# Squares of the first feed-forward layer on ScalarE, its sums on VectorE, a smaller stock of weight planes, and head blocks squared one per group

## The chip, the cores and the metric

The kernel runs on one core of one Trainium2 chip. The metric is the device time of one execution in microseconds (us). Three executions of the kernel before took 1282.55, 1283.82 and 1284.52 us, so its median is 1283.82 us.

## The reference

An encoder block: layer norm, an input projection, two attention branches (a two-dimensional neighbourhood attention and a windowed grouped attention), gating, an output projection, a second layer norm, and a squared-ReLU MLP. The change touches the stretch from the output projection to the end of the MLP's first layer:

```
attn_out = mixed @ w_out + b_out
h = layer_norm(ALPHA * h + attn_out, ln1_g, ln1_b)
u = jnp.square(jax.nn.relu(h @ w_ff1 + b_ff1))      # first layer, 1024 -> 4096
ffn_out = u @ w_ff2 + b_ff2                         # second layer, 4096 -> 1024
h = layer_norm(ALPHA * h + ffn_out, ln2_g, ln2_b)
```

There are 1024 tokens of width 1024.

## The kernel before

All five engines follow an order that is written out in the program: each engine takes its instructions in that order, and waits where a semaphore asks for it.

**Output projection (`out_mm`, TensorE, about 560 to 660 us).** It goes in eight groups g of 128 tokens. Each group has two halves of 24 matmuls. Between the two quarters of the second half stand the eight transposes of the group before, `turn(g - 1)` (L1374), which need that group normalised (`normalise`, L176, on ScalarE, after statistics on VectorE and a power on GpSimd). `turn_evac` takes the transposes out of PSUM (six of eight on ScalarE, L1385), and `combine` turns the tokens into the first layer's operands.

**First layer (`ff1_mm`, L1471).** It is done by Strassen's method in Winograd's form: for each of 16 blocks p of 256 hidden units there are seven products i, in the order `STEPS` = 1, 2, 6, 5, 7, 3, 4. One product is 12 matmuls of 128x512 in float16, because each operand is held as a high and a low plane. The weight planes of a product are made by ScalarE (`hi1`, L1673, a scaled copy) and VectorE (`lo1`, L1677, the rest); for products 6, 5, 7 and 4 VectorE first makes a sum of weight blocks (`sums1`, L1647 and L1662). `tick()` makes the planes of one product, and `prep_to(n)` ticks until the stock reaches product n. The table `PREP` says up to where for the first products, a formula with `LOOK` for the later ones. Blocks 0 to 3 are the head blocks: their products 1 and 2 run between the last groups of the projection, and their weights lie in the upper halves of the operand tiles (`raws`, loaded by `head_w`). The remaining products stand in `seq`: (0,6), (1,6), (0,5), (1,5), (0,7), (0,3), (0,4), (1,7), (1,3), (1,4), then 6, 5, 7, 3, 4 of blocks 2 and 3, then all seven of blocks 4 to 15. I write (p,i) for product i of block p, and n for its place in `seq`.

**Scales.** A block's weights are scaled by their norm: `squares1` (L1423, ScalarE, one 128x2048 instruction), a tiny matmul (L1428), `scale1` on VectorE (L1433) and GpSimd (L1434).

**Results.** `snap` (L1562, ScalarE) copies a partial sum out of PSUM, which lets the next product accumulate into that bank. `act_fn` adds a second partial sum to it on VectorE (L1581), and `settle()`, one or two products later, runs the rest: max with zero and square in one VectorE instruction (L1584), and the store. The fourth result (A21) has its ReLU and square on ScalarE (L1578, L1579). `u_sums` makes four sums of the squared blocks for the second layer, one after each of the next products (two in block 1), on GpSimd (L1685).

**Second layer (L1937).** It starts when the last products of block 15 are out; its operands are loaded, and cast by ScalarE (L1799) and VectorE (L1802).

Of the kernel before, what the change touches and what calls it, by code (L numbers as in the profile page):

```python
# [13 lines left out]
AF = mybir.ActivationFunctionType  # L14
ALU = mybir.AluOpType
# [46 lines left out]
LO_ON = (2, 3, 4, 5), (1, 3, 5)  # L62
RS = 3, 3.5, 4.5, 5.5
HI_AT = -1
PREP = 5, 6, 7, 8, 8, 9, 11, 12, 13, 14, 15, 17, 18, 20, 22
HI_ACT = (2, 3, 4, 5), ()
ST0=2
NO_DVE = ()
# [22 lines left out]
def encoder_block(ctx, tc, x, w_in, w_br, w_out, w_ff1, w_ff2, par, rows, rpbp,  # L91
                  ident_d, masks_d, rope_d, out):
    nc = tc.nc
    PE, ACT, DVE, POOL = nc.tensor, nc.scalar, nc.vector, nc.gpsimd
# [61 lines left out]
    def dma_w(src):  # L156
        raw = wp.tile([P, 8, P], F32, tag="raw", name="raw", bufs=2)
        nc.sync.dma_start(raw, src)
        return raw
# [633 lines left out]
    with tc.manual_schedule(engines=MANUAL):  # L793
        raws = [dma_w(gate_w(i, 8 - N_AHEAD)) for i in range(2)]
# [480 lines left out]
        for f in range(8):  # L1275
            for half in range(2):
# [8 lines left out]
                g, h = (f, 1) if half == 0 else (f + 1, 0)  # L1285
# [26 lines left out]
    raws = {}  # L1312
# [109 lines left out]
    def squares1(p, raw):  # L1422
        ACT.activation(junk1, raw.rearrange("p r c k n -> p (r c k n)"), AF.Square, accum_out=sq1[:, p:p + 1],  # L1423
                       saturate=False)

    def sum_sq1(p, tag):
        ps = psum(tag)
        PE.matmul(ps[:, 0:2], ones, sq1[:, p:p + 1].to_broadcast([P, 2]), start=True, stop=True)  # L1428
        return ps

    def scale1(p, ps):
        t = tw1[:, 2 * p:2 * p + 2]
        DVE.scalar_tensor_tensor(out=t, in0=ps[:, 0:2], scalar=Q_MIN, in1=cv, op0=ALU.max, op1=ALU.mult)  # L1433
        POOL.tensor_tensor(out=sw1[:, 2 * p:2 * p + 2], in0=t, in1=pw, op=ALU.pow)  # L1434
# [14 lines left out]
    def head_w(p):  # L1449

        nc.sync.dma_start(raws[p], w_ff1[p])
# [36 lines left out]
    with tc.manual_schedule(engines=MANUAL):  # L1488
# [10 lines left out]
        for g in range(NCG):  # L1499
            out_mm(g, 0, 0, 8)  # L1500
            if 2 <= g + 1 < NCG:
                split_mx(g + 1)
            if g + 2 < NCG:
                pre(g + 2)
            out_evac(g, 0)
            out_mm(g, 1, 0, 4)
            if g:
                turn(g - 1)
            out_mm(g, 1, 4, 8)
            if g == 4:  # L1510
                head_ps = [sum_sq1(p, "o") for p in range(2)]
            if g == 7:
                head_ps += [sum_sq1(p, "o") for p in range(2, 4)]
            if g:
                turn_evac(g - 1)
            if g == 3:
                for p in range(2):
                    squares1(p, raws[p])
            if g == 5:
                head_split(0, 1)  # L1520
                head_split(0, 2)
            if g == 6:
                for p in range(2, 4):
                    squares1(p, raws[p])
            out_evac(g, 1)
            if g == 0:
                bound(bound_sum())
            ln1_norm(g)
            if g < 5:
                late(g + 3)  # L1530
            if g == 5:
                op_places("S1", "S2")
            if g:
                combine(g - 1)
            if g == 2:
                for p in range(2):
                    head_w(p)
            if g == 4:
                for p in range(2):
                    scale1(p, head_ps[p])  # L1540
            if g == 5:
                for p in range(2, 4):
                    head_w(p)
            if g == 6:
                head_split(1, 1)
                head_split(1, 2)
            if g == 7:
                for p in range(2, 4):
                    scale1(p, head_ps[p])
# [24 lines left out]
        def act_fn(p, i, n, ps, add, f):  # L1574

            u = us[p, n] = ufree.pop(0)
            if add is None:
                ACT.activation(u, ps, AF.Relu, bias=f_bias(p, f), scale=w_back(p))  # L1578
                ACT.activation(u, u, AF.Square)  # L1579
                return  # L1580
            DVE.scalar_tensor_tensor(out=u, in0=ps, scalar=w_back(p), in1=add, op0=ALU.mult, op1=ALU.add)  # L1581

            def rest_of():
                DVE.scalar_tensor_tensor(out=u, in0=u, scalar=0.0, in1=u, op0=ALU.max, op1=ALU.mult)  # L1584
                store_u(p, i, u)
            waiting.append(rest_of)

# [47 lines left out]
        raw1, sums = {}, {}  # L1635
# [44 lines left out]
        def u_sums(p):  # L1680

            u11, u12, u21, u22 = (us[p, n] for n in ("A11", "A12", "A21", "A22"))

            def one(i, out, a, b, op=ALU.subtract):
                POOL.tensor_tensor(out=out, in0=a, in1=b, op=op)  # L1685
                store_u(p, i, out)
            return [lambda: one(7, u11, u11, u21), lambda: one(5, u21, u21, u22, ALU.add),
                    lambda: one(6, u22, u22, u11),
                    lambda: (one(3, u12, u12, u22), ufree.extend((u11, u21, u22, u12)))]
# [25 lines left out]
        def prep_to(n):  # L1715
            while n_prep[0] < min(n, len(seq)):
                tick()
# [46 lines left out]
        def residual_rows1():  # L1764
            for r in range(2):
                nc.sync.dma_start(xts[0][:, r, :], rr_d[2 + r].partition_broadcast(P))
# [117 lines left out]
                tring.insert(0, slot2("q2"))  # L1884

        tails = []
        LOOK = 9
        n_res = 0
        for n, (p, i) in enumerate(seq):
            prep_to(PREP[n] if n < len(PREP) else n + min(LOOK, 5 + n // 3))  # L1890
            if n == 0:
                comb_hi("A22")
            elif n == 1:
                comb_lo("A22")
            elif n == 2:
                more_tw()
            if n == 12:
                xts.append(x1p.tile([P, 2, D], F32, tag="m", name="rr"))
                xts.append(x0p.tile([P, 4, 512], F32, tag="m", name="rst"))
                residual_rows1()  # L1900
            if n in (11, 14):
                scale1(n // 3 + 1, sum_sq1(n // 3 + 1, "s"))
            ff1_mm(p, i)
            if n in (8, 11):
                squares1(n // 3 + 2, raw1[n // 3 + 2])
            if (p, i) == (NP - 1, 6):

                t = hp.tile([P, 2, 4, 512], F32, tag="h3", name="stg")
                gring.extend(t[:, x] for x in range(2))
                load_s(0)  # L1910
            for f in tails[:2 if p == 1 else 1]:
                tails.pop(0)()
            after1(p, i)
            if p == NP - 1:
                turn_over(i)
            if i == 4:
                tails.extend(u_sums(p))
            if n > 12 and n % 4 == 0 and n_res < 2 * NCG + 2:
                if n_res >= 2:
                    residual()  # L1920
                if n_res < 2 * NCG:
                    residual_load(n_res, xn1_d)
                n_res += 1
# [141 lines left out]
        for n in range(L3):  # L2065
            i = idx(n)
# [150 lines left out]
```

## Time and profile before

| quantity | value |
|---|---|
| median of three executions | 1283.82 us |
| the profiled execution | 1282.07 us |
| its span, first to last instruction | 1280.3 us |
| TensorE busy | 1249.4 us, 98% |
| VectorE busy | 993.2 us, 78% |
| ScalarE busy | 703.9 us, 55% |
| GpSimd busy | 409.1 us, 32% |
| mean granted TensorE clock | 0.998 |

A row of the timeline gives the start in us from the span's start, the duration, the engine, the source line, the operation, output and input tiles, the shape, and a count; in square brackets stands how long the engine was idle before it, and which instruction ended that idle time. PE is TensorE, DVE is VectorE, ACT is ScalarE, POOL is GpSimd, SPq is SyncE's DMA queue. Instructions of one engine overlap by 0.08 to 0.16 us, so the distance from start to start is the price of one in a row of them.

### The profile page before, as it was taken

The numbers are of one execution on the slowest core, as the hardware profiler recorded it, in microseconds if no ns is written. First come the engines' busy times: TensorE is split into PE (matmuls) and PEld (weight loads), VectorE is DVE, ScalarE is ACT, GpSimd is POOL, SyncE is SP. The second block draws the span as 40 slices with busy tenths as digits, with TensorE's granted clock in tenths as the row PEclk, the third lists the DMA queues.
The fourth block names the chain that finished last, engine by engine and source line by source line (L and its number), as shares of the span: only waits on it lengthen the run. The fifth ranks groups of instructions, "written<-read, shape, count | busy, mean of one in ns | idle before, by whom it ended". The sixth has DMA issues, their size and how long they took to land.

```text
span 1280.3 us, 16490 instructions
## 1 busy us (share of the span) xinstructions
PE 1249.4 (98%) x5946; PEld 915.5 (72%) x5946; DVE 993.2 (78%) x1369; ACT 703.9 (55%) x1088; POOL 409.1 (32%) x372
## 2 busy tenths in 40 slices
PE   8999999999999999999998999999999999999997
PEld 6788887877778788888773444444447888888885
DVE  7667889777778964445679989999958677797778
ACT  6448778667675455424556655555535542333346
POOL 4343322112110003437510457676632001111207
PEclk9999999999999999999999999999999999999999
DMA  6535667465566326552442466566547644534223
GB/s 235 169 127 142 155 156 163 112 157 126 129 146 194 109 106 235 189 186 105 182 155 75 143 201 214 206 215 206 173 148 285 251 158 168 221 143 179 107 107 132
DMA packets 166066, 211.55 MB, mean 165 GB/s; under 512 B 110432, under 2 KB 112224, under 8 KB 159712
## 3 DMA queue, kind: packets, MB, share of 16 engines
q1 hardware_dynamic: 165152, 209.72, 50.8%
q8 instruction: 46, 0.75, 0.3%
q10 hardware_dynamic: 832, 0.79, 0.2%
q14 instruction: 36, 0.29, 0.1%
HBM read 128.59 MB, written 56.18 MB: 144 GB/s over the span
## 4 chain that ended last, share of the span: by engine, by line
PE 76%; DVE 11%; ACT 4%; issue 3%; DMA 2%; POOL 2%; SPq 1%; DVEq 0%; POOLq 0%; ACTq 0%
PE ps_mm L316 17%; PE ps_mm L1937 7%; PE ps_s L1937 6%; PE ps_mm L1471 5%; PE ps_t L1471 5%; PE ps_o L1937 5%; PE ps_o L1471 5%; PE ps_t L1937 5%; PE ps_s L1471 2%; PE ps_o L744 2%; PE ps_mm L977 2%; PE ps_o L308 1%; PE ps_t L308 1%; PE ps_t L306 1%; PE ps_o L307 1%
## 5 line engine op out<-in xcount | busy, mean ns | idle before, releaser
L316 PE MATMUL ps_mm<-hT,whi 128*128 128x512 f32 x832 | 269.7, 398 | 6.6 <-DVE kl L429 4.0
L1471 PEld LDWEIGHTS <-tw 128*128 128x128 f16 x1248 | 122.0, 99 | 149.0 <-issue 4.1
L316 PEld LDWEIGHTS ps_mm<-hT,whi 128*128 128x128 f32 x832 | 155.2, 188 | 41.1 <-ACT ss L659 3.9
L316 PE MATMUL ps_mm<-hT,wlo 128*128 128x512 f32 x416 | 165.5, 398 | 1.0 <-DVE wlo L810 1.0
L1685 POOL TENSOR_TENSOR usl<-usl 128x512 f32<-128x512 f32 x64 | 100.3, 1567 | 120.4 <-ACT usl L1579 112.0
L659 ACT ACTIVATE ss<-ss,sk 128x384 f32<-128x384 f32 (+1 forms) x128 | 74.3, 582 | 57.7 <-DVE sk L641 34.5
L1799 ACT CAST t<-stg 128x2048 fp32r<-128x2048 f32 x28 | 53.6, 1913 | 81.8 <-PE ps_o L1937 46.4
L1956 POOL TENSOR_TENSOR acc<-acc,rst 128x512 f32<-128x512 f32 x16 | 28.0, 1749 | 212.8 <-DMA rst<-xr_d 184.7
L1937 PE MATMUL ps_mm<-t,t 128*128 128x512 f32 x384 | 89.9, 390 | 0.0
L1269 POOL TENSOR_TENSOR mx<-sg 128x512 f32<-128x512 f32 x16 | 33.5, 2091 | 176.4 <-DVE sg L1268 176.4
L1937 PE MATMUL ps_s<-t,t 128*128 128x512 f32 x384 | 89.6, 389 | 0.0
L316 PEld LDWEIGHTS ps_mm<-hT,wlo 128*128 128x128 f32 x416 | 78.3, 188 | 14.0 <-DVE wlo L810 1.5
L1471 PE MATMUL ps_t<-hS,tw 128*128 128x512 f16 x372 | 85.4, 379 | 1.8 <-ACT sn L1562 1.7
L1937 PEld LDWEIGHTS ps_mm<-t,t 128*128 128x128 f32 x384 | 72.0, 188 | 15.2 <-DVE t L1802 0.2
L1937 PEld LDWEIGHTS ps_s<-t,t 128*128 128x128 f32 x384 | 72.1, 188 | 14.9
L1802 DVE TENSOR_TENSOR t<-stg,t 128x2048 fp32r<-128x2048 f32 x28 | 66.9, 2388 | 12.1 <-ACT t L1799 12.1
L1677 DVE SCALAR_TENSOR_TENSOR tw<-ts,c,tw 128x512 f16<-128x512 f32 x61 | 72.0, 1185 | 2.8 <-ACT tw L1673 2.7
L1937 PE MATMUL ps_t<-t,t 128*128 128x512 f32 x288 | 67.8, 390 | 0.6 <-DVE t L1802 0.6
L1937 PE MATMUL ps_o<-t,t 128*128 128x512 f32 x288 | 67.2, 389 | 0.0
L1673 ACT ACTIVATE tw<-ts,c 128x512 f16<-128x512 f32 x61 | 43.4, 714 | 36.5 <-DVE ts L1647 20.9
L1937 PEld LDWEIGHTS ps_t<-t,t 128*128 128x128 f32 x288 | 53.9, 188 | 12.6 <-DVE t L1802 1.5
L1937 PEld LDWEIGHTS ps_o<-t,t 128*128 128x128 f32 x288 | 54.1, 188 | 11.2
(343 smaller groups left out, 2848.6 us busy)
## 6 DMA issues: line engine op xcount, KB each, us to landing
us_d<-usl SPq DMA_DIRECT2D x112, 256.0 KB, 2.7
stg<-us_d SPq DMA_DIRECT2D x28, 1024.0 KB, 4.9
raw<-in_w_in SPq DMA_DIRECT2D x28, 512.0 KB, 4.2
raw<-in_w_ff SPq DMA_DIRECT2D x24, 512.0 KB, 5.5
sg<-sg_d SPq DMA_DIRECT2D x32, 256.0 KB, 3.3
w2b<-in_w_ff SPq DMA_DIRECT2D x7, 1024.0 KB, 6.8
w2a<-in_w_ff SPq DMA_DIRECT2D x5, 1024.0 KB, 6.9
sg_d<-sa SPq DMA_DIRECT2D x16, 256.0 KB, 2.2
```

The costliest lines, as they stand in the source:

```text
L308: PE.matmul(ps, lo[:, k0 + k, :], act(0, k), start=False, stop=l)
L316: PE.matmul(ps, a[:, k, :], act(b, k), start=(k == 0 and i == 0), stop=(k == NK - 1 and i == 2))
L659: ACT.activation(p, p, AF.Exp, bias=nm[:, i:i + 1], scale=0.125, accum_out=sums_l[o_chunk][:, hh, 2 * t + i:2 * t + i + 1])
L1269: POOL.tensor_tensor(out=mx[:, f, half * 512:(half + 1) * 512], in0=both[0], in1=both[1], op=ALU.add)
L1471: PE.matmul(ps, ww, act[:, part, k, :], start=(first and k == 0 and m == 0), stop=(k == 3 and m == 2), skip_group_check=True)
L1673: ACT.activation(hi_lo(slot, 0), source1(p, i), AF.Copy, bias=0.0, scale=w_scale(p))
L1677: DVE.scalar_tensor_tensor(out=hi_lo(slot, 1), in0=source1(p, i), scalar=w_scale(p), in1=hi_lo(slot, 0), op0=ALU.mult, op1=ALU.subtract)
L1685: POOL.tensor_tensor(out=out, in0=a, in1=b, op=op)
L1799: ACT.copy(slot[:, :, 0, :], src)
L1802: DVE.tensor_tensor(out=slot[:, :, 1, :], in0=src, in1=b32(slot[:, :, 0, :]), op=ALU.subtract)
L1937: PE.matmul(ps, st[:, a, part, j * P:(j + 1) * P], w[:, a, wpart, :], start=(first and a == 0 and m == 0), stop=(a == 3 and m == 2), skip_ ...
L1956: POOL.tensor_tensor(out=z, in0=z, in1=t, op=ALU.add)
```

## The change

It has four parts.

1. The VectorE instruction of `settle()` (max and square, 48 in all) becomes two on ScalarE, Relu and Square.
2. The 64 sums of `u_sums` go from GpSimd to VectorE.
3. The stock of weight planes is smaller: `PREP` is lower from its seventh entry on, and the stock grows from five products ahead at n = 12 to seven at n = 24, where it went to nine. The norms of blocks 4 and 5 (`squares1`, `scale1`) move three products later.
4. The first two head blocks are loaded in groups 0 and 1 (both in group 2 before) and squared in groups 2 and 3 (both in group 3 before).

```diff
-PREP = 5, 6, 7, 8, 8, 9, 11, 12, 13, 14, 15, 17, 18, 20, 22
+PREP = 5, 6, 7, 8, 8, 9, 10, 12, 13, 14, 15, 16
...
-            if g == 3:
-                for p in range(2):
-                    squares1(p, raws[p])
+            if 2 <= g < 4:
+                squares1(g - 2, raws[g - 2])
...
-            if g == 2:
-                for p in range(2):
-                    head_w(p)
+            if g < 2:
+                head_w(g)
...
             def rest_of():
-                DVE.scalar_tensor_tensor(out=u, in0=u, scalar=0.0, in1=u, op0=ALU.max, op1=ALU.mult)
+                ACT.activation(u, u, AF.Relu)
+                ACT.activation(u, u, AF.Square)
                 store_u(p, i, u)
...
             def one(i, out, a, b, op=ALU.subtract):
-                POOL.tensor_tensor(out=out, in0=a, in1=b, op=op)
+                DVE.tensor_tensor(out=out, in0=a, in1=b, op=op)
                 store_u(p, i, out)
...
-        LOOK = 9
+        LOOK = 7
...
-            prep_to(PREP[n] if n < len(PREP) else n + min(LOOK, 5 + n // 3))
+            prep_to(PREP[n] if n < len(PREP) else n + min(LOOK, 3 + n // 6))
...
-            if n in (11, 14):
-                scale1(n // 3 + 1, sum_sq1(n // 3 + 1, "s"))
-            ff1_mm(p, i)
-            if n in (8, 11):
-                squares1(n // 3 + 2, raw1[n // 3 + 2])
+            if n in (14, 17):
+                scale1(n // 3, sum_sq1(n // 3, "s"))
+            ff1_mm(p, i)
+            if n in (11, 14):
+                squares1(n // 3 + 1, raw1[n // 3 + 1])
```

The lines after the edit stand one to two numbers lower in the changed kernel (L1579 is now what L1581 was; L1582 and L1583 are Relu and Square; L1646, L1672, L1676 and L1684 were L1647, L1673, L1677 and L1685).

**ScalarE, groups 2 and 3 of the projection.** `junk` is what the squares of a head block (hA_5402 is block 0, hA_5403 block 1) write besides their sum; `zl<-zl,mv` is the normalisation of that group.

```order
 L1236 CAST m<-mx 128x1024
 L1385 ACTIVATE mx<-ps_t,c_5405 128x128 x6
+L1423 ACTIVATE junk,c_5405<-hA_5402 128x2048
 L176 ACTIVATE zl<-zl,mv 128x1024
 L1390 CAST hA_5402<-mx 128x4x128
```

```order
 L1236 CAST m<-mx 128x1024
 L1385 ACTIVATE mx<-ps_t,c_5405 128x128 x6
-L1423 ACTIVATE junk,c_5405<-hA_5402 128x2048
 L1423 ACTIVATE junk,c_5405<-hA_5403 128x2048
 L176 ACTIVATE zl<-zl,mv 128x1024
```

Block 0's squares have gone from group 3 to group 2, each time ahead of a normalisation.

**ScalarE, the opening of the first layer, before and then now**, from the cast of the operand of product 3 to the high plane of (0,4). `sn` is a snapshot, `tw` and `twx` are slots of weight planes, the CASTs make operands.

```order
L1720 CAST hS_6199<-mx 128x2048
L1562 ACTIVATE sn<-ps_o,prm,c_5405 128x512
L1673 ACTIVATE tw_5404<-ts,c_5405 128x512
L1673 ACTIVATE twx<-ts,c_5405 128x512
L1673 ACTIVATE twx<-hA_5402,c_5405 128x512
L1720 CAST hA_6200<-mx 128x2048
L1562 ACTIVATE sn<-ps_mm,prm,c_5405 128x512
L1673 ACTIVATE twx<-ts,c_5405 128x512
```

```order
L1719 CAST hS_6199<-mx 128x2048
L1560 ACTIVATE sn<-ps_o,prm,c_5405 128x512
L1582 ACTIVATE usl<-usl 128x512
L1583 ACTIVATE usl<-usl 128x512
L1672 ACTIVATE tw_5404<-ts,c_5405 128x512
L1672 ACTIVATE twx<-ts,c_5405 128x512
L1672 ACTIVATE twx<-hA_5402,c_5405 128x512
L1719 CAST hA_6200<-mx 128x2048
L1560 ACTIVATE sn<-ps_mm,prm,c_5405 128x512
L1582 ACTIVATE usl<-usl 128x512
L1583 ACTIVATE usl<-usl 128x512
L1672 ACTIVATE twx<-ts,c_5405 128x512
```

Two pairs of Relu and Square now stand between a snapshot and the next high plane, so that plane and every later snapshot wait for them.

**VectorE, some 30 us later, before and then now**, from the sum for (2,4) to the sums of block 3. `usl` holds results and squares.

```order
L1662 TENSOR_TENSOR ts<-hS_5983,ts 128x512
L1584 SCALAR_TENSOR_TENSOR usl<-usl 128x512
L1581 SCALAR_TENSOR_TENSOR usl<-ps_t,c_5405,sn 128x512
L1677 SCALAR_TENSOR_TENSOR tw_6436<-hS_5983,c_5405,tw_6436 128x512
L1647 TENSOR_TENSOR ts<-hS_5984 128x512
L1647 TENSOR_TENSOR ts<-hS_5984,ts 128x512
L1584 SCALAR_TENSOR_TENSOR usl<-usl 128x512
L1677 SCALAR_TENSOR_TENSOR tw_6436<-ts,c_5405,tw_6436 128x512 x2
```

```order
L1661 TENSOR_TENSOR ts<-hS_5983,ts 128x512
L1684 TENSOR_TENSOR usl<-usl 128x512 x2
L1579 SCALAR_TENSOR_TENSOR usl<-ps_t,c_5405,sn 128x512
L1676 SCALAR_TENSOR_TENSOR tw_6440<-hS_5983,c_5405,tw_6440 128x512
L1646 TENSOR_TENSOR ts<-hS_5984 128x512
L1646 TENSOR_TENSOR ts<-hS_5984,ts 128x512
L1676 SCALAR_TENSOR_TENSOR tw_6440<-ts,c_5405,tw_6440 128x512
L1684 TENSOR_TENSOR usl<-usl 128x512
```

The squares (L1584) are gone from VectorE and the sums that GpSimd made (L1684) stand in their places, each waiting for squares that now come from ScalarE.

## The prediction

> **What bounds the kernel now.** I read the page's first part, then the busy time by stretches, then TensorE's idle times, and then what each of those waited for.
>
> ```profile
> PE 1249.4 (98%) x5946; PEld 915.5 (72%) x5946; DVE 993.2 (78%) x1369; ACT 703.9 (55%) x1088; POOL 409.1 (32%) x372
> ```
>
> TensorE is busy for 98% of the span at full clock, so nothing but its idle time is to be had: 30.9 us, most of it outside the changed stretch. The next fence is the busy time by stretches, first layer's opening first, then one stretch of its steady part (columns: window, its length, busy us of each engine, clock, DMA).
>
> ```profile
> 680.00:690.00 10.00, 8.24 (x37) 3.42 (x36) 9.73 (x14) 7.73 (x10) 0.00 (x0) 1.00 0.14 53
> 690.00:700.00 10.00, 9.22 (x43) 4.05 (x43) 9.97 (x12) 5.81 (x8) 0.00 (x0) 1.00 0.14 54
> 700.00:710.00 10.00, 7.51 (x35) 3.32 (x34) 9.18 (x15) 5.64 (x9) 0.00 (x0) 1.00 0.07 26
> 710.00:720.00 10.00, 10.00 (x49) 4.73 (x48) 10.00 (x10) 5.64 (x8) 7.68 (x5) 1.00 0.43 158
> 720.00:730.00 10.00, 7.75 (x38) 3.52 (x36) 8.66 (x13) 7.73 (x11) 5.34 (x4) 1.00 0.40 102
> ```
>
> ```profile
> 800.00:900.00 100.00, 100.00 (x471) 46.17 (x470) 96.99 (x102) 56.76 (x78) 66.22 (x45) 1.00 0.60 205
> ```
>
> From 750 us on TensorE has no gap, although VectorE is 97% busy: the first layer's steady part is bound by TensorE, and a lighter VectorE gains nothing there. In the opening TensorE loses 7.28 us in the five stretches shown (10 minus its busy time in each), while VectorE is nearly full. ScalarE has room there: 32.6 of 50 us are busy. TensorE's larger gaps are these:
>
> ```profile
> 622.45 1.09 PE L1374 MATMUL ps_t<-ident,zl 128*128 128x128 f32 x8 [2.20 <-ACT zl L176]
> ...
> 679.54 0.61 PE L1471 MATMUL ps_o<-hA,twx 128*128 128x512 f16 x2 [0.61 <-ACT twx L1438]
> 680.99 2.33 PE L1471 MATMUL ps_o<-hA,twx 128*128 128x512 f16 x10 [0.84 <-DVE twx L1439]
> 684.24 2.75 PE L1471 MATMUL ps_s<-hA,twx 128*128 128x512 f16 x12 [0.92 <-DVE usl L1581]
> ...
> 690.64 2.33 PE L1471 MATMUL ps_mm<-hS,tw 128*128 128x512 f16 x10 [0.62 <-DVE tw L1677]
> ...
> 703.56 2.75 PE L1471 MATMUL ps_t<-hS,twx 128*128 128x512 f16 x12 [2.49 <-ACT sn L1562]
> ...
> 722.57 2.75 PE L1471 MATMUL ps_o<-hS,tw 128*128 128x512 f16 x12 [0.58 <-ACT sn L1562]
> 726.99 2.75 PE L1471 MATMUL ps_t<-hS,tw 128*128 128x512 f16 x12 [1.67 <-ACT sn L1562]
> ...
> 743.74 1.46 PE L1471 MATMUL ps_o<-hA,tw 128*128 128x512 f16 x6 [0.61 <-DVE usl L1581]
> ```
>
> The bracketed times give 2.20 us at 622 and 8.34 us in the opening; two more of 0.16 and 0.15 us (rows not shown) make 8.65. So the most that the change can take away is 10.9 us.
>
> **The head squares (part 4).** The 2.20 us at 622 wait for a normalisation on ScalarE:
>
> ```profile
> 603.62 1.24 ACT L176 ACTIVATE zl<-zl,mv 128x1024 f32<-128x1024 f32 x1 [4.23 <-POOL mv L174]
> ...
> 615.62 1.91 ACT L1423 ACTIVATE junk<-hA 128x2048 fp8e5<-128x2048 f32 x1 [4.46 <-DMA hA<-in_w_ff]
> ...
> 619.26 1.91 ACT L1423 ACTIVATE junk<-hA 128x2048 fp8e5<-128x2048 f32 x1 [1.64 <-DMA hA<-in_w_ff]
> ...
> 621.17 1.22 ACT L176 ACTIVATE zl<-zl,mv 128x1024 f32<-128x1024 f32 x1
> ```
>
> ```profile
> 615.20 0.27 POOL L174 TENSOR_SCALAR mv<-mv 128x1 f32<-128x1 f32 x1
> ```
>
> ```profile
> 584.68 8.74 SPq L1365 DMA_DIRECT2D xn_d<-z  x2
> ...
> 610.00 1.19 SPq L1451 DMA_DIRECT2D hA<-in_w_ff  x2
> ```
>
> GpSimd has the statistics ready at 615.47, but ScalarE stands at the squares of two head blocks, which wait 4.46 and 1.64 us for their loads; the normalisation starts at 621.17 and not at 615.5. The loads were issued at 610.0 and 610.6 and were usable at 615.6 and 619.3, at most 8.7 us later. Now each is issued behind the stores of groups 0 and 1, whose two rows start at 584.68 and end at 593.4. On SyncE's queue they move past the stores of groups 1 and 2 and one store of residual rows, which nothing on the path waits for, and they have 14 and 17 us until their squares. One square (1.91 + 0.10 us) stands ahead of each normalisation; in group 3 it runs from 611.2 and is done at 613.2, ahead of 615.5, and in group 2 it falls into the 4.23 us of idle time ahead of 603.62. TensorE reaches the transposes at 620.25; the normalisation is done by 616.8. Gain: 2.2 us; if a load were late, none (0). What is late next there is nothing: I find no other gap until 679.
>
> **The squares and sums (parts 1 and 2), in the opening.** What one costs, and who disturbs whom:
>
> ```profile
> 686.97 0.75 DVE L1581 SCALAR_TENSOR_TENSOR usl<-ps_s,c,sn 128x512 f32<-128x512 f32 x1 [0.20 <-ACT sn L1562]
> 687.64 2.28 DVE L1723 TENSOR_TENSOR hS<-mx,hS 128x2048 f16<-128x2048 f32 x1
> ...
> 706.79 0.68 DVE L1584 SCALAR_TENSOR_TENSOR usl<-usl 128x512 f32<-128x512 f32 x1
> 707.40 0.75 DVE L1581 SCALAR_TENSOR_TENSOR usl<-ps_t,c,sn 128x512 f32<-128x512 f32 x1
> ...
> 713.95 1.75 DVE L1662 TENSOR_TENSOR ts<-hS,ts 128x512 f32<-128x512 f32 x1
> 715.62 1.75 DVE L1584 SCALAR_TENSOR_TENSOR usl<-usl 128x512 f32<-128x512 f32 x1
> ```
>
> ```profile
> 710.46 6.37 POOL L1685 TENSOR_TENSOR usl<-usl 128x512 f32<-128x512 f32 x4 [39.07 <-ACT usl L1579]
> ```
>
> ```profile
> 708.94 0.78 ACT L1578 ACTIVATE usl<-ps_mm,prm,c 128x512 f32<-128x512 f32 x1 [0.69 <-PE ps_mm L1471]
> 709.75 0.63 ACT L1579 ACTIVATE usl<-usl 128x512 f32<-128x512 f32 x1
> ```
>
> A VectorE instruction with two operands in SBUF takes 0.68 us alone and 1.75 us while GpSimd runs the sums (713.95 and 715.62 lie inside the four sums of 710.46 to 716.83). A square costs VectorE 0.61 us undisturbed (706.79 to 707.40). A sum costs GpSimd 1.59 us, and VectorE loses 1.07 us for each instruction that it hits; on VectorE it costs about 0.61 us, the price of the like instruction there. Relu and Square on SBUF, f32, aren't in the trace as a pair; the nearest is the second of L1578 and L1579, 0.63 us, so a pair is 1.26 us. (Bounds: 1.07, if starts overlap as L1579's successors do, and 1.44, the L1578 pair out of PSUM.)
>
> I now place the changed order row by row from 680 us, with these prices and each engine's order:
>
> - (3,2), gap 0.92: it waits for a bank that L1581 empties, and one square stood right ahead of that. It leaves: the gap is 0.3. Gain 0.6.
> - (1,6), gap 0.62: its low plane stands on VectorE behind the operand's remainder (687.64), which stands behind L1581 (686.97), which already waits for ScalarE's snapshot. The slot of the second square turns into waiting (1.3 us), the plane comes only 0.2 us earlier, and TensorE arrives 0.6 us earlier: gap 1.1. Loss 0.5.
> - (0,3), gap 2.49:
>
> ```profile
> 702.12 0.72 ACT L1673 ACTIVATE twx<-ts,c 128x512 f16<-128x512 f32 x1 [3.28 <-DVE ts L1647]
> 702.75 0.76 ACT L1562 ACTIVATE sn<-ps_t,prm,c 128x512 f32<-128x512 f32 x1
> ...
> 721.13 0.72 ACT L1673 ACTIVATE tw<-ts,c 128x512 f16<-128x512 f32 x1 [2.93 <-DVE ts L1647]
> ...
> 724.28 1.89 ACT L1423 ACTIVATE junk<-raw 128x2048 fp8e5<-128x2048 f32 x1
> ...
> 726.18 0.76 ACT L1562 ACTIVATE sn<-ps_t,prm,c 128x512 f32<-128x512 f32 x1
> ```
>
> The snapshot at 702.75 stands behind the high plane at 702.12, which waits for a VectorE sum. Four squares have left VectorE by then (2.4 us), of which 1.3 go into the wait above; the sum comes 1.5 us earlier in absolute time, though four pairs (5.0 us) were put into ScalarE, because they fall into its idle times. That plane starts at 700.6, the snapshot ends at 702.0 and (0,3) starts at 702.05. So here TensorE stands 1.5 us earlier than before.
> - (2,7) and (2,3), gaps 0.58 and 1.67: both snapshots are late because of VectorE sums that ran at 1.75 us, and the second also because the squares of block 4 (1.89 us) stand ahead of it. GpSimd is silent there now. By my placing the snapshots end at 719.1 and 722.4, and TensorE arrives at 720.2 and 722.8: both gaps go, the second by only 0.4 us. Gain 2.25.
> - (3,7) and (3,4), 0.15 and 0.61: VectorE is by then two to three us ahead. Gain 0.76.
>
> Opening: 1.5 + 2.25 + 0.76 = 4.5 us. Its bounds: nothing (ScalarE's pairs eat it all) and 8.65.
>
> **The steady part and the smaller stock (parts 1 to 3).** In the chain of what ended last a product is one piece:
>
> ```profile
> 749.08 2.59 PE ps_s L1471 x12
> ```
>
> Seven products take 7 x 2.59 = 18.1 us of TensorE. VectorE has 17 instructions of about 0.64 us for them, 10.9 us; that it is 97% busy (17.6 us) is GpSimd's doing. Now it has 18, 11.5 us, and about 3.5 GpSimd instructions of the residual rows remain, 3.7 us: 15.2 of 18.1. ScalarE goes from 57% (10.3 us) to 14.1 of 18.1 with three pairs more. Both stay under TensorE, so the cost is 0, covered by TensorE's own work. The new waits are VectorE's: a sum of the fourth result waits for TensorE and then 1.4 us of ScalarE, and the low planes of the coming products are queued behind it. With five products in stock that is 4 x 2.59 = 10.4 us of cover; without the cover each block would cost 1.4 us, 12 blocks 17 us. The scales of blocks 4 and 5, whose squares come three products later, are ready by my placing 4 us before the first plane that needs them, since GpSimd's power no longer queues behind sums; cost 0. A stock of five instead of nine also spares VectorE and ScalarE planes in the opening.
>
> **The change to the second layer.** TensorE starts there just when its first operand is ready, so a delay would count in full:
>
> ```profile
> 956.70 1.90 ACT L1799 CAST t<-w2a 128x2048 fp32r<-128x2048 f32 x1 [0.82 <-DMA w2a<-in_w_ff]
> ```
>
> ```profile
> 963.04 2.29 DVE L1802 TENSOR_TENSOR t<-stg,t 128x2048 fp32r<-128x2048 f32 x1 [1.45 <-ACT t L1799]
> ```
>
> The second row makes the operand's low part just as TensorE is due to use it; it waits for ScalarE's second cast, which waits for a load. One new pair stands ahead of the first cast, whose load ended its wait at 956.70, and makes that cast some 0.4 us late; none stands between the second load and its cast. Cost 0, at most 0.4.
>
> **Sum.** 1282.07 - 2.2 - 4.5 = 1275.4 for an execution like the profiled one (its span 1280.3 plus 1.8 around it). That execution is 1.75 us below the median of three; against the median I predict 1283.8 - 6.7 = 1277.1, rounded to 1277.0.
>
> **Rivals.** Within 0.2% (2.6 us) a measurement of this kernel can't tell from no change.
>
> A. *As forecast*, 3.5 to 8 us off: 1275.8 to 1280.3, at its likeliest 1277.0. Chance 0.62.
>
> B. *The opening doesn't gain.* ScalarE's pairs stand ahead of the planes and snapshots, and VectorE's waits for snapshots take the place of its squares, as already at (1,6). Then only the head squares count: 1281.6. For it: my margins at (2,3) are 0.4 us. Against it: 17.4 us of idle ScalarE in the 50 us shown. Chance 0.15, a third of which still clears 0.2%.
>
> C. *ScalarE's order becomes the bound of the opening: slower.* Ten pairs stand ahead of the snapshot or plane that TensorE waits for until 730 us. It decides from 6.7 / 10 = 0.67 us more per pair than I put, 1.93 us: then everything gained is given back. If half the pairs lie on the chain in full (6.3 us) and only the head's 2.2 us are gained, the time is 1283.8 + 4.1 = 1287.9. Against it: L1578 and L1579 are the same two functions, 0.81 us from start to start, with nothing between them. Chance 0.11. The Trainium skill ("ScalarE: Activation LUTs", "Rules for kernel authors") says to use VectorE, not ScalarE, for relu and multiplication, since VectorE is the faster per element. By that rule this case comes true, with its 1287.9; the rows agree on the price of one (0.68 against 1.26 us), but they show VectorE full and ScalarE not.
>
> D. *All gaps go*: with GpSimd quiet VectorE gets so far ahead that the gaps at 679 to 703 close too: 1283.8 - 10.9 = 1272.9. Against it: the first two (0.61 and 0.84) come from the last group's planes, which the change doesn't touch. Chance 0.12.
>
> Faster by over 0.2%: A, D and a third of B, 0.79, less a little for A's edge: 0.77. The same: 0.12. Slower: 0.11. The range reaches from D (1272.8) to just past B, 1283.0.
>
> **What would show it.** Right: no gap before the transposes of group 3; at (0,3) a gap of about 1.7 us; none at (2,7), (2,3) and (3,4); VectorE's two-operand rows at 0.68 us between 710 and 755 us; VectorE near 84% and ScalarE near 78% in the steady part; no gap of TensorE there. Wrong: Relu or Square well above 0.63 us, VectorE idle behind L1582 or L1583 with a TensorE gap behind it, or gaps at low or high planes after block 4.

## The result and the profile after

The changed kernel takes 1275.22 us (median of four executions, 1274.73 to 1275.76); the kernel before takes 1284.08 us beside it (1282.55 to 1284.52). The ratio is 0.9933, with a 95% interval of 0.9916 to 0.9950: faster by 8.9 us, or 0.7%, by the medians. The two profiled executions differ by less, 1282.07 against 1275.46 us: 6.6 us, against the 6.7 of the forecast's sum. The second half of this story finds the source of about 1 of the other 2.3 us; the rest stays open.

First the page's busy time, and busy time by stretches, in the same windows as before:

```profile
PE 1248.5 (98%) x5946; PEld 915.2 (72%) x5946; DVE 953.1 (75%) x1385; ACT 758.1 (60%) x1184; POOL 313.0 (25%) x308
```

```profile
680.00:690.00 10.00, 8.63 (x40) 3.71 (x39) 8.68 (x12) 9.04 (x11) 0.00 (x0) 1.00 0.14 54
690.00:700.00 10.00, 8.51 (x40) 3.75 (x39) 9.21 (x10) 8.19 (x13) 0.00 (x0) 1.00 0.14 54
700.00:710.00 10.00, 9.88 (x46) 4.50 (x46) 8.37 (x14) 8.29 (x14) 0.00 (x0) 1.00 0.16 60
710.00:720.00 10.00, 10.00 (x48) 4.53 (x47) 9.89 (x16) 8.28 (x13) 0.00 (x0) 1.00 0.52 188
720.00:730.00 10.00, 10.00 (x49) 4.71 (x48) 6.47 (x12) 9.84 (x16) 1.13 (x1) 1.00 0.79 232
800.00:900.00 100.00, 100.00 (x472) 46.16 (x470) 80.36 (x108) 74.48 (x111) 31.51 (x24) 1.00 0.64 218
```

TensorE loses 2.98 us in the first five windows, where it lost 7.28, and nothing from 701 us on. ScalarE is busy for 43.6 of these 50 us, which took 32.6 before: the work went into its idle time. In the steady part VectorE is at 80%, ScalarE at 74%, and TensorE has no gap, as before. TensorE's gaps between 560 and 950 us are now these:

```profile
585.68 1.09 PE L1374 MATMUL ps_t<-ident,z 128*128 128x128 f32 x8 [0.64 <-ACT z L176]
...
678.93 2.33 PE L1471 MATMUL ps_o<-hA,twx 128*128 128x512 f16 x10 [0.84 <-DVE twx L1439]
681.58 2.75 PE L1471 MATMUL ps_s<-hA,twx 128*128 128x512 f16 x12 [0.32 <-DVE usl L1579]
...
688.40 2.33 PE L1471 MATMUL ps_mm<-hS,tw 128*128 128x512 f16 x10 [1.05 <-DVE tw L1676]
...
700.12 2.75 PE L1471 MATMUL ps_t<-hS,twx 128*128 128x512 f16 x12 [1.62 <-ACT sn L1560]
```

They add up to 4.47 us, against 10.85 before: 6.38 of the 6.6 us. The first gap is new, but the change has not begun there: the first instruction that it moves is this load of a head block, behind the gap's end.

```profile
586.07 0.38 SPq L1451 DMA_DIRECT2D hA<-in_w_ff  x1
```

Nor is the gap in two kernels below with the same code there (without part 1, without part 3). And the 0.61 us that stood at 679.54 is absent here, while it came back in another kernel with the same code there (the one with two steps moved). The two cancel.

### The profile page after: what moved, and what is told of

The parts are those of the page before. It is cut to its first block, busy times and chain, and to the rows that moved or that the text cites. A ratio compares the mean times of both kernels' runs of the same rounds, so it can differ in the third digit from the quotient of the medians.

```text
span 1273.7 us, 16525 instructions
## 1 busy us (share of the span) xinstructions
PE 1248.5 (98%) x5946; PEld 915.2 (72%) x5946; DVE 953.1 (75%) x1385; ACT 758.1 (60%) x1184; POOL 313.0 (25%) x308
## 4 chain that ended last, share of the span: by engine, by line
PE 75%; DVE 12%; ACT 5%; issue 3%; DMA 2%; POOL 2%; SPq 1%; DVEq 0%; POOLq 0%; ACTq 0%
PE ps_mm L316 17%; PE ps_mm L1936 7%; PE ps_s L1936 6%; PE ps_t L1471 6%; PE ps_o L1471 6%; PE ps_mm L1471 6%; PE ps_o L1936 5%; PE ps_t L1936 5%; PE ps_s L1471 2%; PE ps_o L744 2%; PE ps_mm L977 2%; PE ps_o L307 1%; PE ps_t L307 1%; PE ps_o L308 1%; PE ps_t L308 1%
## 5 line engine op out<-in xcount | busy, mean ns | idle before, releaser
L1955 POOL TENSOR_TENSOR acc<-acc,rst 128x512 f32<-128x512 f32 x16 | 30.7, 1918 | 262.8 <-DMA rst<-xr_d 234.8
L1684 DVE TENSOR_TENSOR usl<-usl 128x512 f32<-128x512 f32 x64 | 52.6, 821 | 25.7 <-ACT usl L1577 25.5
L1434 POOL TENSOR_TENSOR c<-c 128x2 f32<-128x2 f32 x16 | 17.3, 1086 | 193.6 <-DVE c L1433 193.6
L1672 ACT ACTIVATE tw<-ts,c 128x512 f16<-128x512 f32 x61 | 43.2, 712 | 27.3 <-DVE ts L1646 27.3
```

The source lines that it names most:

```text
L1672: ACT.activation(hi_lo(slot, 0), source1(p, i), AF.Copy, bias=0.0, scale=w_scale(p))
L1684: DVE.tensor_tensor(out=out, in0=a, in1=b, op=op)
L1955: POOL.tensor_tensor(out=z, in0=z, in1=t, op=ALU.add)
```

## The experiments

Each experiment has the kernel before measured beside it (medians 1284.0, 1284.4 and 1284.0 us in the three groups of runs), so times can be set side by side.

### One part alone

**The head squares alone (part 4).**

```diff
-            if g == 3:
-                for p in range(2):
-                    squares1(p, raws[p])
+            if 2 <= g < 4:
+                squares1(g - 2, raws[g - 2])
...
-            if g == 2:
-                for p in range(2):
-                    head_w(p)
+            if g < 2:
+                head_w(g)
```

> The kernel before with the head blocks' loads and squares moved (part 4) and nothing else. My theory: the 2.2 us gap before the transposes of group 3 goes, the opening keeps its 8.65 us of gaps: 2.2 to 2.5 us faster than before. Rival (the gap moves on, because ScalarE is late somewhere else): within 1 us of before, and a new gap between 600 and 680 us.

Measured: 1280.24 us (1279.06 to 1282.93), ratio 0.9970 (0.9958 to 0.9981). The gap at 622 is gone and the gaps of the opening stand as before, (0,3) with its 2.49 us; only the smallest, of 0.15 us, is absent. By the medians it gained 3.8 us (2.4 to 5.4 by the ratio's interval), more than the 2.2 that its gap was long.

**The squares alone (part 1).**

```diff
-                DVE.scalar_tensor_tensor(out=u, in0=u, scalar=0.0, in1=u, op0=ALU.max, op1=ALU.mult)
+                ACT.activation(u, u, AF.Relu)
+                ACT.activation(u, u, AF.Square)
```

> The kernel before with Relu and Square on ScalarE (part 1) and nothing else; GpSimd still makes the sums. My theory (VectorE bounds the opening, and squares and sums each take a part of its load): gaps of 0.3, 1.1 and 1.6 us at (3,2), (1,6), (0,3) as in the changed kernel, and half of the later 3.0 us stays because VectorE is still hit by GpSimd: 2 to 3 us faster. Rival G (only GpSimd's silence counts, ScalarE's pairs eat what VectorE wins): 0 to 1 us faster, with gaps at (2,7) and (2,3) as before. Rival S (the smaller stock counts): no change.

Measured: 1279.97 us (1279.29 to 1281.73), ratio 0.9967 (0.9955 to 0.9979), 4.1 us by the medians (2.7 to 5.8 by the interval), where I expected 2 to 3. Up to (0,3) its gaps are the changed kernel's (.31, 1.05 and 1.62 us). Behind (0,3) its timeline keeps half of what was there:

```profile
702.71 2.75 PE L1471 MATMUL ps_t<-hS,twx 128*128 128x512 f16 x12 [1.62 <-ACT sn L1562]
...
724.17 2.75 PE L1471 MATMUL ps_t<-hS,tw 128*128 128x512 f16 x12 [0.44 <-ACT sn L1562]
...
735.52 2.75 PE L1471 MATMUL ps_o<-hS,tw 128*128 128x512 f16 x12 [0.69 <-ACT sn L1562]
...
741.22 2.75 PE L1471 MATMUL ps_o<-hA,tw 128*128 128x512 f16 x12 [0.36 <-DVE usl L1581]
```

**The sums alone (part 2).**

```diff
-                POOL.tensor_tensor(out=out, in0=a, in1=b, op=op)
+                DVE.tensor_tensor(out=out, in0=a, in1=b, op=op)
```

> The kernel before with the sums on VectorE (part 2) and nothing else. My theory: the gaps up to (0,3), 4.6 us with the first ones, stay, since GpSimd is silent there anyway; those from (2,7) on (3.0 us) go or nearly go: 2 to 3 us faster. Rival G: 4.5 us faster. Rival S: no change. In the steady part VectorE falls from 97% to some 88%.

Measured: 1281.38 us (1280.30 to 1283.00), ratio 0.9980 (0.9970 to 0.9989), 2.65 us. Up to (0,3) the gaps are those of before, and behind it only this one of 0.24 us is left of 3.0:

```profile
726.67 2.75 PE L1471 MATMUL ps_t<-hS,tw 128*128 128x512 f16 x12 [0.24 <-ACT sn L1562]
```

With GpSimd silent, VectorE's two-operand rows there stay at 0.68 us. In the steady part VectorE is at 81%, where I expected some 88%.

**The smaller stock alone (part 3).**

```diff
-PREP = 5, 6, 7, 8, 8, 9, 11, 12, 13, 14, 15, 17, 18, 20, 22
+PREP = 5, 6, 7, 8, 8, 9, 10, 12, 13, 14, 15, 16
...
-        LOOK = 9
+        LOOK = 7
...
-            prep_to(PREP[n] if n < len(PREP) else n + min(LOOK, 5 + n // 3))
+            prep_to(PREP[n] if n < len(PREP) else n + min(LOOK, 3 + n // 6))
...
(and the norms of blocks 4 and 5 three products later)
```

> The kernel before with the smaller stock and the later squares of blocks 4 and 5 (part 3) and nothing else. My theory: up to (0,3) nothing changes; behind it VectorE has a plane or two less to make and the squares of block 4 no longer stand ahead of a snapshot, so 1 us of the 3.0 goes: 0.5 to 1.5 us faster, unless VectorE, 97% busy, can't fill the smaller stock, which would show as gaps after 760 us and make it slower. Rival S: 4 us faster or more.

Measured: 1285.28 us (1282.16 to 1286.30), ratio 1.0004 (0.9996 to 1.0013). It saves 1.0 us behind (0,3), where 2.0 of 3.0 are left:

```profile
725.51 2.75 PE L1471 MATMUL ps_o<-hS,tw 128*128 128x512 f16 x12 [1.59 <-ACT sn L1562]
728.68 1.67 PE L1471 MATMUL ps_t<-hS,tw 128*128 128x512 f16 x7 [0.42 <-ACT sn L1562]
```

It gives 0.8 back in four gaps of .17 to .23 us in the steady part, where VectorE is still 91% busy and a smaller stock covers less. That is a tie, where I expected 0.5 to 1.5 us. (Of the table `PREP` the change lowers only the seventh entry and those from the twelfth on; the four between are the same.)

### One part left out

**Without part 1** (square on VectorE).

> The changed kernel with the square left on VectorE. Theory (the opening waits for VectorE's walk order, and the 1.22 us square stands in that walk): the gaps .92, .62, .16 and 2.49 of before return, the gaps at (2,7) and (2,3) stay small; with the head's 2.2 gone the kernel is about 1279 to 1280 us, some 4 to 5 us above the changed kernel's 1275.2, and in executions where the granted clock falls behind the 2.49 us gap some 1.6 us more. Rival (the sums or the stock carry the gain of the opening): within 1.5 us of the changed kernel.

Measured: 1277.40 us (1276.34 to 1277.54), 2.2 us above the changed kernel, half of what I expected. I had added all 4.19 us of the four returning gaps to the changed kernel's time, which already holds 2.99 us of gaps in their place; and no row shows a square at 1.22 us: it takes VectorE 0.68, and 1.22 us is VectorE's wait in the changed kernel. All its gaps between 680 and 760 us, from its timeline:

```profile
682.01 2.75 PE L1471 MATMUL ps_s<-hA,twx 128*128 128x512 f16 x12 [0.92 <-DVE usl L1579]
688.40 2.33 PE L1471 MATMUL ps_mm<-hS,tw 128*128 128x512 f16 x10 [0.62 <-DVE tw L1675]
693.92 2.33 PE L1471 MATMUL ps_t<-hS,tw 128*128 128x512 f16 x10 [0.16 <-DVE tw L1675]
701.32 2.75 PE L1471 MATMUL ps_t<-hS,twx 128*128 128x512 f16 x12 [2.49 <-ACT sn L1560]
```

They are the four of before, 4.19 us against 2.99 in the changed kernel: the squares are worth 1.2 us of gaps, and they lie up to (0,3). (The one run at the changed kernel's clock of .998 is 1.1 us above it; the other three are at .997.) Behind (0,3) nothing is left, without the squares' help.

**Without part 2** (sums on GpSimd).

> The changed kernel with the sums of A11, A12, A21, A22 left on GpSimd. Theory: the gaps up to (0,3) are those of the changed kernel (.84, .32, 1.05, 1.62), and of the gaps behind it some 1.5 us come back at (2,3), (3,7) and (3,4), where VectorE's work meets GpSimd's sums as in the kernel with the squares alone: about 1276.7 us, 1 to 2 us above the changed kernel. Rival (the sums carry no time of their own once the squares are off VectorE): the same as the changed kernel, 1275.2 within 0.7 us.

Measured: 1275.86 us (1275.12 to 1276.27), 0.6 us above the changed kernel. There is no gap behind (0,3) in the first layer. My theory's 1.5 us did not come back; the rival was right.

**Without part 3** (the old stock).

> The changed kernel with the old stock of weight planes (up to nine, squares of the weight block ahead at the old products). Theory (the stock bought nothing, and the alone-run of it was flat): 1275.2 within 1 us; the only place where it can cost is (2,3), where the squares of block 4 stand ahead of a snapshot with 0.4 us to spare, so at most 0.5 us there. Rival (the stock's later start of the planes is what took away the 1.67 us at (2,3) or the 0.61 at (3,7)): 1.5 to 2.5 us above the changed kernel, with a gap at one of these places.

Measured: 1275.63 us (1274.71 to 1276.32), 0.4 us above, and no gap behind (0,3) either.

So, by one trace of each kernel, the 3.0 us behind (0,3) are taken away by any two of the three parts; alone, the squares take 1.5, the sums 2.8 and the stock 1.0. What no other part replaces is the head's 2.2 us and the squares' 1.2 us up to (0,3): 2.2 + 1.2 + 3.0 = 6.4.

### Where the medians' other two microseconds come from

The head squares and the squares alone gained more by the medians (3.8 and 4.1 us) than the gaps that they took away (2.2, and 1.2 + 1.5). Both cut a long pause. The trace of the sums alone shows why (the product behind the pause of 2.49 us, then the granted clock in two windows, the eighth column):

```profile
703.87 4.29 PE L1471 MATMUL ps_t<-hS,twx 128*128 128x512 f16 x12 [2.49 <-ACT sn L1562]
```

```profile
700.00:705.00 5.00, 2.51 (x10) 0.93 (x9) 4.21 (x6) 2.56 (x4) 0.00 (x0) 0.86 0.00 1
705.00:710.00 5.00, 5.00 (x20) 2.09 (x19) 4.56 (x8) 2.05 (x4) 0.00 (x0) 0.80 0.14 52
```

The same product takes 2.75 us in the profiled execution of the kernel before; here it takes 4.29, because the clock fell behind the pause. In the fourteen profiled executions, taken in windows of 5 us, up to 1260 us the clock is below .985 in four places only, and each is directly behind a pause of 2.13 to 2.49 us at 622 or at (0,3) (shorter pause and stock alone at 622; sums alone and stock alone at (0,3)). Seven other pauses of 1.91 to 3.09 us at these two places have no fall behind them. Two kernels test that this belongs to the pauses.

**The changed kernel with a longer pause.**

```diff
             slot = tws[p, i] = take()
+            if (p, i) == (1, 7):
+                DVE.tensor_tensor(out=sums[p, 7], in0=b1(p, 2, 2), in1=b1(p, 1, 2), op=ALU.subtract)
+                ACT.activation(hi_lo(slot, 0), source1(p, i), AF.Copy, bias=0.0, scale=w_scale(p))
             ACT.activation(hi_lo(slot, 0), source1(p, i), AF.Copy, bias=0.0, scale=w_scale(p))
```

> The changed kernel in which two steps ahead of the snapshot that product (0,3) waits for, the sum and the high part of plane (1,7) (0.68 us on VectorE and 0.62 to 0.71 us on ScalarE in its trace), are each done twice, with the same values. TensorE's pause ahead of (0,3) should grow from 1.62 us to about 2.9. Theory (a pause of 2.5 us or more lets the granted clock fall in part of the executions): 1276.4 us where it does not fall, 1278 where it does; a mean clock of .997 or below in part of the runs, and a spread over 1.5 us where the changed kernel's four runs spread by 1.0. Rival (the lower clock in some runs has nothing to do with the pause): the pause alone, 1276.5 within 0.7 us, mean clock .998 in all runs and product (0,3) at 2.75 us.

Measured: 1277.34 us (1276.00 to 1279.01); two of five runs have a mean clock of .997 and .996, and the spread is 3.0 us. The profiled execution shows the pause at 3.09 us with the product behind it at 2.75: the clock falls in some executions, not in all.

```profile
702.29 2.75 PE L1471 MATMUL ps_t<-hS,twx 128*128 128x512 f16 x12 [3.09 <-ACT sn L1560]
```

The spread of the times proves less than I meant it to. The profiled execution took 1278.64 us at a mean clock of .998, 2.2 us more than I gave an execution without a fall; its trace has 1.7 us more idle time of TensorE ahead of 560 us than the changed kernel's, and 0.9 us at the start of the second layer, and the edit touches neither place.

**The kernel before with a shorter pause.**

```diff
-PREP = 5, 6, 7, 8, 8, 9, 11, 12, 13, 14, 15, 17, 18, 20, 22
+PREP = 5, 6, 6, 8, 8, 9, 11, 12, 13, 14, 15, 17, 18, 20, 22
```

> The kernel before with plane (1,7) prepared one product later, behind the snapshot that (0,3) waits for. Theory: the pause of 2.49 us ahead of (0,3) becomes shorter than 2 us, and what is saved there is paid back at the next products (VectorE has the same work in the same stretch), so that without a fall of the clock nothing is won: every run at a mean clock of .998, near 1282 to 1282.8, which is the kernel before's time in its executions at .998, and 1 to 2 us under its median. Rival (order, not work, sets the opening): the pause shrinks by 1 to 1.5 us, nothing comes back, 1280.5 to 1281.5. Rival (the fall of the clock is not tied to this pause): runs at .995 to .997 as before, median 1283.5 to 1284.5.

Measured: 1283.56 us (1281.15 to 1284.37), ratio 0.9994 (0.9985 to 1.0003). The pause at (0,3) went, 1.35 us came at the product behind it, and the opening's gaps sum to 6.87 us, 7.20 before: as expected. But I expected every run at .998, and 10 of 11 are at .996 or .997, with the median where the second rival put it (the fall is not tied to this pause). What no run shows any more is .995, which 9 of 46 runs of the kernel before have; with 11 runs that could still be chance. Its trace shows the place that I had overlooked, the pause of part 4 at 622, which this edit leaves (the transposes behind it, and matmuls ahead of and behind them):

```profile
619.98 0.39 PE L1347 MATMUL ps_s<-wo,m 128*128 128x512 f32 x1
622.53 1.09 PE L1374 MATMUL ps_t<-ident,zl 128*128 128x128 f32 x8 [2.17 <-ACT zl L176]
...
623.73 0.63 PE L1346 MATMUL ps_s<-wo,m 128*128 128x512 f32 x1
624.16 0.63 PE L1347 MATMUL ps_s<-wo,m 128*128 128x512 f32 x1
...
627.34 0.39 PE L1346 MATMUL ps_s<-wo,m 128*128 128x512 f32 x1
```

```profile
620.00:625.00 5.00, 2.83 (x14) 2.11 (x13) 1.81 (x3) 5.00 (x8) 0.78 (x1) 0.86 0.35 142
625.00:630.00 5.00, 5.00 (x21) 4.12 (x20) 4.38 (x9) 1.55 (x5) 0.00 (x0) 0.79 0.45 173
630.00:635.00 5.00, 5.00 (x24) 4.14 (x23) 2.20 (x2) 3.23 (x4) 4.75 (x5) 1.00 0.26 105
```

Until about 627 us the matmuls follow each other at 0.43 us, and then at 0.23 again. Sorted by how many pauses over 1.9 us a kernel's profile has between 560 and 760 us, the mean granted clocks of all runs are as follows. The line at 1.9 us is a close one: the shortest pause above it is 1.91 us (sums alone, at 622, with no fall behind it), the longest below it 1.86.

| pauses over 1.9 us | kernels | runs | at .997 or less | at .996 or less | at .995 |
|---|---|---|---|---|---|
| two (622 and (0,3)) | before, sums alone, stock alone | 67 | 52 | 34 | 18 |
| one | head alone, squares alone, without part 1, shorter pause, longer pause | 32 | 20 | 10 | 0 |
| none | changed kernel, without part 2, without part 3, and the three below | 27 | 3 | 0 | 0 |

The mean time of the kernel before is 1285.4 us over its 9 runs at .995 and 1283.1 us over its 11 runs at .998 (46 runs in these three groups). So the two pauses cost their own length, 4.69 us together, and up to about 2.3 us more behind them, where the clock fell most.

This does not account for all of the difference between the medians' 8.9 us and the profiled executions' 6.6. The mean of all 46 runs of the kernel before is 1284.1 us, so runs in which the clock fell raise it by 1.0 us above the 1283.1. Another 1.0 us is that the profiled execution (1282.07) was faster than the average run at its own clock, and 0.2 us that the changed kernel's was slower than its median. At .998 alone the kernel before averages 1283.1, the head alone 1279.7 (four runs), the squares alone 1279.5 (three) and the changed kernel 1275.2 (four): gains of 3.4, 3.6 and 7.9 us for gaps of 2.2, 2.7 and 6.4. What the remaining 0.9 to 1.5 us are isn't shown; one trace of each kernel can't say how long a gap is in the other executions.

### What is left in the opening: order or amount of work?

**Two steps moved in the changed kernel.**

```diff
-PREP = 5, 6, 7, 8, 8, 9, 10, 12, 13, 14, 15, 16
+PREP = 5, 6, 6, 8, 8, 9, 10, 12, 13, 14, 15, 16
...
-        comb_lo("S3")
         ff1_mm(3, 1)
         tick()
+        comb_lo("S3")
```

> The changed kernel with two steps moved, to cut its two longest gaps: plane (1,7) is prepared one product later, behind the snapshot that product (0,3) waits for, and one low-part combination of the opening is put behind product (3,1) and the walk after it. Theory (both gaps, 1.05 and 1.62 us, come from VectorE steps ahead of what TensorE waits for): the first falls below .4 and the second below .5, together 1.5 to 2.7 us, so 1272.5 to 1273.7 us. Rival (what was late moves to the next product: the plane moved is missed at (1,7), or the combination's buffer at the next transpose): a new gap of about 1 us each, and a time within 0.7 us of 1275.2.

Measured: 1274.69 us (1274.04 to 1275.41), 0.5 us under the changed kernel, with overlapping ranges. The gaps of 1.05 and 1.62 are gone, and in their place stand these:

```profile
693.13 2.33 PE L1471 MATMUL ps_t<-hS,tw 128*128 128x512 f16 x10 [0.78 <-DVE tw L1676]
701.33 2.75 PE L1471 MATMUL ps_mm<-hA,twx 128*128 128x512 f16 x12 [0.68 <-DVE usl L1579]
710.01 2.75 PE L1471 MATMUL ps_mm<-hA,tw 128*128 128x512 f16 x12 [0.76 <-DVE usl L1579]
```

2.22 us for 2.67: the rival was right, the wait moves to the next products.

**Work taken from VectorE: four or all eight sums of weight blocks 0 and 1 on GpSimd** (the first edit with `i == 7` added to its condition for the four).

```diff
-            DVE.tensor_tensor(out=t, in0=a, in1=b, op=ALU.subtract)
+            (POOL if p < 2 else DVE).tensor_tensor(out=t, in0=a, in1=b, op=ALU.subtract)
...
-                    DVE.tensor_tensor(out=t, in0=b1(p, 2, 1), in1=t, op=ALU.subtract)
+                    (POOL if p < 2 else DVE).tensor_tensor(out=t, in0=b1(p, 2, 1), in1=t, op=ALU.subtract)
```

> The changed kernel with four of the sums of weight blocks in the opening (planes (0,7), (1,7), (0,4), (1,4)) on GpSimd, which does nothing between 670 and 725 us. Theory (the opening waits for VectorE's amount of work): the gap of 1.62 us at (0,3) falls below .6 and 1.05 at (1,6) stays: 1.0 to 1.4 us, so 1273.8 to 1274.3. Rival (GpSimd's 1.5 us for a sum makes the plane late instead): a new wait of 0.5 to 1 us on ScalarE's high part of (1,7) or (1,4), and 1275.2 within 0.5 us.

> The same with all eight sums of the first two blocks' planes on GpSimd, 5.5 us off VectorE between 679 and 703 us. Theory: the gaps .32, 1.05 and 1.62 all fall, to .8 or less together, so 2.2 to 3 us: 1272.2 to 1273.0, and faster than any kernel here. Rival (eight sums one after the other on GpSimd, 12 us, come too late for the planes (1,6) and (0,5)): waits on ScalarE's high parts for GpSimd, 1 to 3 us of new gaps, 1274.5 to 1276.

Measured: 1274.86 us (1274.25 to 1275.64) with four and 1274.33 us (1273.53 to 1274.69) with eight. With four the gap of 1.62 fell to .99, not below .6, and a new one of .31 stands ahead of it: within the rival's range. The kernel with eight is the fastest here, 0.9 us under the changed one; their ranges don't meet, but the intervals of their ratios to the kernel before do (0.9912 to 0.9939). It is a third of what I expected, and its trace shows both hands of the trade: the gaps, VectorE's planes ahead of the first of them, and GpSimd's sums at that time (all with eight).

```profile
678.62 2.33 PE L1471 MATMUL ps_o<-hA,twx 128*128 128x512 f16 x10 [1.86 <-DVE twx L1439]
...
694.32 2.75 PE L1471 MATMUL ps_mm<-hS,twx 128*128 128x512 f16 x12 [0.25 <-ACT sn L1560]
698.05 2.32 PE L1471 MATMUL ps_t<-hS,twx 128*128 128x512 f16 x10 [0.98 <-ACT sn L1560]
```

```profile
676.80 3.44 DVE L1439 SCALAR_TENSOR_TENSOR twx<-hS,c,twx 128x512 f16<-128x512 f32 x2
```

```profile
676.45 1.56 POOL L1646 TENSOR_TENSOR ts<-hA,ts 128x512 f32<-128x512 f32 x1 [5.78 <-DVE mx L1408]
677.97 1.72 POOL L1646 TENSOR_TENSOR ts<-hA 128x512 f32<-128x512 f32 x1
```

The gaps of .32 and 1.05 are gone and 1.62 became .98, but two planes that took VectorE 1.41 us in the changed kernel take 3.44 beside GpSimd, and their gap grew from .84 to 1.86. A further 1.11 us appeared at the start of the second layer; gaps of 0.5 to 1.2 us stand there in seven of the fourteen profiled executions and none in the other seven, with and without the parts of the change, and I did not find what sets them.

## Why the prediction was right, and where it was off

- **The head squares, 2.2 us.** Right. ScalarE's rows of the changed kernel show one square ahead of each normalisation, and the normalisation again waits for GpSimd and not for a load:

```profile
612.02 1.93 ACT L1423 ACTIVATE junk<-hA 128x2048 fp8e5<-128x2048 f32 x1
...
616.46 1.25 ACT L176 ACTIVATE zl<-zl,mv 128x1024 f32<-128x1024 f32 x1 [2.41 <-POOL mv L174]
```

- **The opening, row by row.** 4.5 us predicted, 4.2 found (1.2 us up to (0,3), where I had 1.5, and 3.0 behind). (3,2): .3 predicted, .32 measured. (1,6): 1.1 predicted as a loss, 1.05. (0,3): about 1.7, 1.62. But these three gaps don't fit the 1.5 us that went into my sum: with .3, 1.1 and 1.7 in place of .92, .62, .16 and 2.49 TensorE gains 1.1 us up to (0,3), and 1.2 were measured. (2,7), (2,3), (3,7) and (3,4): 0, and 0. Product (3,4) starts at 736.65 us where it started at 743.74.
- **The price of a pair.** Taken as 1.26 us from the nearest row; it is 1.19 us from start to start, and the wait that I put into VectorE's walk behind it is there (1.22 us at 684.73):

```profile
684.60 0.62 ACT L1582 ACTIVATE usl<-usl 128x512 f32<-128x512 f32 x1
685.25 0.63 ACT L1583 ACTIVATE usl<-usl 128x512 f32<-128x512 f32 x1
685.79 0.71 ACT L1672 ACTIVATE tw<-ts,c 128x512 f16<-128x512 f32 x1
```

```profile
684.73 0.75 DVE L1579 SCALAR_TENSOR_TENSOR usl<-ps_s,c,sn 128x512 f32<-128x512 f32 x1 [1.22 <-ACT sn L1560]
...
711.51 1.41 DVE L1684 TENSOR_TENSOR usl<-usl 128x512 f32<-128x512 f32 x2
```

- **VectorE undisturbed.** The second row above is two sums, 0.7 us each, where rows of this kind took 1.75 us beside GpSimd. (The second of the two rows that I read as lying inside GpSimd's sums ends at 717.37, 0.5 us after them.)
- **The steady part, 0.** Right; the loads were put at 84% and 78%, a little high (80% and 74%).
- **Credit behind (0,3).** I gave those 3.0 us to GpSimd's silence. The size is right, but the reason is only one of three, any two of which do it: without part 2 they are gone all the same.
- **The sum for the profiled execution.** It gave 1275.4 us, and 1275.46 were measured. That close an agreement is luck: four runs of the changed kernel spread over 1.0 us, the opening came out 0.3 us short, and two gaps outside the forecast, 0.64 and 0.61 us, cancelled.
- **The median.** This is the step that was off. I set the same 6.7 us against the median, which lay 1.75 us higher, as if that offset would stay, and so came to 1277.0, 1.8 us too high; the median measured lies 0.6 us below the lower end of my case A. A part of the offset belonged to the two pauses, which the change shortens: the profiled execution of the kernel before was one in which the clock did not fall behind them, and such runs average 1283.1 us, 0.7 us under the median that I started from. The other 1.0 us, by which they lie above the profiled execution, is open.
- **Rivals.** B is refuted by the squares alone, which gain 1.2 us up to (0,3) and 1.5 behind. C did not come: ScalarE has the pairs, and no gap grew for them except the one at (1,6) that I had booked. The Trainium skill's rule that I set beside it ("ScalarE: Activation LUTs", "Rules for kernel authors") agrees with the trace on the price of the whole, 1.19 us for a pair against 0.68 us on VectorE. But VectorE did both steps in one instruction; taken singly ScalarE's were no slower, 0.62 and 0.63 us. And the time went the other way, because VectorE was full there. D is refuted by the 3.8 us of gaps left at 679 to 700, and the moved steps, whose saving came back at the next products, point to the reason: VectorE's work fills that stretch.

## What to carry to other kernels

Read a pause of TensorE by its length and by what the clock does behind it: here cutting pauses of 2.2 and 2.5 us to none and to 1.6 was worth more than what was cut, in part because the clock no longer fell behind them. When an engine is full in a stretch, moving a step in its order moves the wait; taking work off helps, but only if the engine that gets it does not slow the first. And leave parts out as well as putting them in alone: three parts that each look worth 1 to 3 us can be covering the same gaps.

## What I had not expected of the hardware

- Behind a pause of 2.13 to 2.49 us TensorE's clock falls in part of the executions: matmuls that start 0.23 us apart then start 0.43 apart for some 3.5 us, which cost 1.54 us at (0,3) in the trace of the sums alone. The Trainium skill ("TensorE: Matmul & The Clock Gate", "HAM oscillation — how this bites in real kernels") puts the limit at gaps over about 3.4 us; the traces here show it below that, and one pause of 3.09 us without it. That the gate's window runs free of the kernel, as the same page says under "What's actually happening", would fit a fall in some executions and not in others; no run here shows the window.
- GpSimd and VectorE slow each other both ways. Two of VectorE's planes took 3.44 us for 1.41 beside GpSimd's sums, and with four sums on GpSimd one of these sums took 3.20 us beside VectorE's operand remainder, where the next ones took 1.72:

```profile
688.80 3.20 POOL L1646 TENSOR_TENSOR ts<-hA 128x512 f32<-128x512 f32 x1 [19.80 <-DVE tw L1676]
```
